# Context products in plain fp32, and ten modulation dots in one buffer ahead of the scan stage

## The chip, the cores and the metric

One Trainium2 chip, one core of it. Times are microseconds (us) of device time; the time of a kernel is the median of its runs. Engines by their names in the profile: PE is TensorE, PEld its weight loads, DVE is VectorE, ACT is ScalarE, SP is the engine on whose queue every transfer of this kernel is issued.

## The reference, cut to what matters

A diffusion backbone of two layers over 1024 latent tokens of width 1024, with 256 context tokens. Layer 0 mixes tokens with a bidirectional gated recurrence (RG-LRU), layer 1 with a short convolution; each is followed by a gated feed-forward. What matters here is the start of layer 0:

```python
sm, cm, gm, sf, cf, gf = adaln(c, ada_w[l], ada_b[l])        # silu(c) @ w + b, six vectors of 1024
smc, cmc, ... = adaln(c_ctx, ada_w[l], ada_b[l])
hl = modulate(rms_norm(x, norm_mix_g[l]), sm, cm)
hc = modulate(rms_norm(h_ctx, norm_mix_g[l]), smc, cmc)
ul = seq_conv(hl @ w_x, ...);  uc = seq_conv(hc @ w_x, ...)   # hc @ w_x: the context products
a, b = rglru_coeffs(u, w_r, b_r, w_i, b_i, lam)              # two small products per block of 256 channels
h_t = a_t * h_{t-1} + b_t                                    # context first, then latent, both directions
yl = (gelu(hl @ w_gate) * (h_fwd + h_bwd)) @ w_out
```

The modulation vectors are products of one vector with 12 x 1024 columns of 1024 weights: 96 groups of 128 results. Each group is one DVE instruction here, a dot product of a 128x1024 tile of weights with the broadcast vector.

## The kernel before

All products work on 128x128 blocks. A full-precision product is made of three passes in fp32r: each operand is split into a high part (ACT rounds it into an fp32r tile) and a low part (DVE subtracts the high part), and `mm` (L436) issues high x high, high x low, low x high into the same PSUM bank. Weights come as 512 KB transfers into raw buffers (three, `raw0`, until the feed-forward opens a fourth) and are split into six slots of 512 columns, `wh` and `wl`. There are four PSUM bank pairs, handed out in turn by `bank` (L208).

The program is a list of units. `run_units` (L369) walks it; ahead of each unit it issues the loads for which a raw buffer is free and the splits for which slots are free, in order of first use. A raw buffer counts as free once its split is recorded. `Plan` (L52) records every instruction and, at each `flush` (L121), writes out all that it recorded since the last one: it plays the instructions through with its own costs, takes at each step the one with the earliest due time among those that could start, and so sets the order in each engine's queue. Engines run their queues in order. So nothing of a later flush comes ahead of anything of an earlier flush on the same engine. The due time of an instruction that nobody in its flush needs is the summed PE cost at its place plus 60 (L134). PE's own order is that of the program.

The stages around the change, by the words of `ORDER` (L45):

- `start` (L567): the first products, with waits on the input.
- `g2`, `shift`, `g3`, `norm`, `g4`, `g5`: gate products of 1024 columns, 48 PE instructions each. `shifts` (L678) convolves three early products into `u` (`u_new`, L732); one of these products, with number 0, stands in `acct`, the 128x1024 tile that later holds square sums and, from here on, serves modulation dots. Then it runs the softplus of the recurrence (`sp` tile).
- `ctx`: `ctx_apply` (L709) makes the modulated context, as `hch` and `hcl`; then eight times `wx_ctx` (L744): 24 PE instructions of 256 columns and a convolution (`conv_a`, L718) of one ACT and three DVE instructions into `uc`.
- `mx`: `open_mx` (L772) flushes, closes the context tiles and opens `mx`, the working tile of the scans.
- `us0`, `e6`, `x4`, `r0`, `d3`, `x5`, `d2`, `r1`, ...: `u_split` (L727) splits `u` and `uc` into `uh`, `ul`; `x4` to `x7` are the remaining products with w_x; `r0` to `r7` (`ri`, L778) are the gates of the recurrence: 60 products that read `uh` and `ul`, then a chain of ACT and DVE instructions and three scans on DVE. `e` and `d` with a number are that many modulation dots (`ahead_dots`, L864): a load of 512 KB and one DVE instruction. `e` puts each in another part of `mx`, `d` puts it in `acct`, so that the load of the next waits for the dot before it.
- Then the output product, the feed-forward, layer 1 and its feed-forward, up to the end. The flush that closes the scan stage is that of `open_ffn` (L910).

Of the kernel before, what the change touches and what calls it, by code (L numbers as in the profile page):

```python
# [8 lines left out]
F32 = mybir.dt.float32  # L9
F32R = mybir.dt.float32r  # L10
AF = mybir.ActivationFunctionType
ALU = mybir.AluOpType

P = 128
D = 1024
KD = 8
SEQ = 1024
HALF = 512
CTX = 256
# [11 lines left out]
for _n, _w in _VEC:  # L31
# [10 lines left out]
DOTS = (0, 0, 0, 1, 1, 2, 2, 2)  # L42


ORDER = ("g2 shift g3 norm g4 g5 ctx mx us0 e6 x4 r0 d3 x5 d2 r1 d2 us2 x6 d1 r2 d1 x7 d1 r3 d1 us4 d1 r4 d1 g6 r5 "  # L45
         "us6 g7 r6 r7")

TABLE = {AF.Silu: (AF.Silu, AF.Tanh), AF.Gelu_apprx_tanh: (AF.Gelu_apprx_tanh, AF.Tanh), AF.Sqrt: (AF.Sqrt,),
         AF.Exp: (AF.Exp, AF.Tanh), AF.Tanh: (AF.Exp, AF.Tanh)}
# [134 lines left out]
def hybrid_kernel(ctx: ExitStack, tc: tile.TileContext, out, xs, cs, c, cc, ada, vecs,  # L184
                  ident, w0, wx, wg, wo, wri, wbi, wbo, wup, wdn):
    nc = Plan(tc)
    V, S, T, G = nc.vector, nc.scalar, nc.tensor, nc.gpsimd
# [28 lines left out]
    def stt(o, a, s, b, op0=ALU.mult, op1=ALU.add, eng=None):  # L216
        (eng or V).scalar_tensor_tensor(out=o, in0=a, scalar=s, in1=b, op0=op0, op1=op1)
# [10 lines left out]
    def act(o, i, f, bias=0.0, scale=1.0):  # L228
        S.activation(o, i, f, bias=bias, scale=scale)
# [24 lines left out]
    x = xp.tile([P, KD, SEQ], F32, tag="x", name="x")  # L254
# [25 lines left out]
    wslots = [(wh0, wl0, i) for i in range(6)]  # L280

    def unit(fn, *keys):
        units.append((fn, keys))
        return len(units) - 1

    class Raw:

        def __init__(self, src, after=-1, pool="raw"):
            self.src, self.after, self.pool, self.left, self.tile = src, after, pool, 0, None

    class Item:

        def __init__(self, key, raws, n, prep, after=-1):
            self.key, self.raws, self.n, self.prep, self.after = key, raws, n, prep, after
            for r in raws:
                r.left += 1

    items = {}

    def wsrc(key):  # L300
        kind = key[0]
        if kind in ("x", "xc"):
            return wx[key[1]]
        if kind == "g":
            return wg[key[1]]
        if kind == "o":
            return wo[key[1]]
        if kind == "ri":
            return wri[key[1]]
        if kind == "bo":  # L310
            return wbo[key[1]]
        return wdn[key[1], key[2], :, 2 * D:]
# [56 lines left out]
    def run_units(nside):  # L369


        stream, seen, last = [], {}, {}
        for i, (_, keys) in enumerate(units):
            for k in keys:
                if k not in seen:
                    seen[k] = i
                    stream.append(items[k] if k in items else weight_item(k))
                    for _ in range(nside(k)):
                        if side:
                            src, dst, bt, eng = side.pop(0)  # L380
                            stream.append(Item(None, [Raw(src)], 0, lambda sl, raws, dst=dst, bt=bt, eng=eng:
                                               dot(dst, raws[0].tile, bt, eng)))
                last[k] = i
        loads = {"raw": [], "s": []}
        for it in stream:
            for r in it.raws:
                if r not in loads[r.pool]:
                    loads[r.pool].append(r)
        free, pos = [True] * 64, 0
        occ, rp = {n: {} for n in loads}, dict.fromkeys(loads, 0)  # L390
        live, np_ = {}, 0
        for i, (fn, keys) in enumerate(units):
            while True:
                moved = False
                for name, todo in loads.items():
                    tiles = raw0 + more.get("raw", []) if name == "raw" else more.get("stage", [])
                    while todo and todo[0].after < i:
                        at = [(rp[name] + j) % len(tiles) for j in range(len(tiles))]
                        at = [j for j in at if j not in occ[name] or not occ[name][j].left]
                        if not at:  # L400
                            break
                        r = todo.pop(0)
                        r.tile = tiles[at[0]]
                        if len(r.src.shape) == 3:
                            nc.sync.dma_start(r.tile.rearrange("p (a b) -> p a b", a=r.src.shape[1]), r.src)
                        else:
                            nc.sync.dma_start(r.tile[:, :r.src.shape[-1]], r.src)
                        occ[name][at[0]] = r
                        rp[name], moved = at[0] + 1, True
                while np_ < len(stream):  # L410
                    it = stream[np_]
                    if it.after >= i or any(r.tile is None for r in it.raws):
                        break
                    n = len(wslots)
                    at = [(pos + j) % n for j in range(n)]
                    at = [j for j in at if j % max(it.n, 1) == 0 and all(free[j:j + it.n])]
                    if not at:
                        break
                    sl = list(range(at[0], at[0] + it.n))
                    if it.n:  # L420
                        pos = (at[0] + it.n) % n
                    for j in sl:
                        free[j] = False
                    for r in it.raws:
                        r.left -= 1
                    live[it.key] = (it.prep([wslots[j] for j in sl], it.raws), sl)
                    np_, moved = np_ + 1, True
                if not moved:
                    break
            fn(*[live[k][0] for k in keys if k[0] != "act"])  # L430
            for k in keys:
                if last[k] == i:
                    for j in live.pop(k)[1]:
                        free[j] = True

    def mm(ps, w, wi, rh, rl, start, stop, **o):  # L436

# [5 lines left out]
    def mmk(ps, w, rhi, rlo, s):  # L443
        n = len(rhi)
        for k in range(n):
            mm(ps[:, s], w, slice(k * P, (k + 1) * P), rhi[k][:, s], rlo[k][:, s], k == 0, k == n - 1)

    def call(fn, *a):
        unit(lambda: fn(*a))
# [97 lines left out]
    cpx = ExitStack()  # L547
    cp = cpx.enter_context(tc.tile_pool(name="cp", bufs=1))
    cs6 = cp.tile([P, 6, CTX], F32, tag="cs6", name="cs6")
    hch = cp.tile([P, KD, CTX], F32R, tag="hch", name="hch")  # L550
    hcl = cp.tile([P, KD, CTX], F32R, tag="hcl", name="hcl")
    xc = cp.tile([P, KD, CTX], F32, tag="xc", name="xc")
    ccb = cp.tile([P, D], F32, tag="ccb", name="ccb")
    uc = up.tile([P, KD, CTX], F32, tag="uc", name="uc")
# [154 lines left out]
    def ctx_apply():  # L709
        make_ab(1, modc, 0, 0, 1, "norm_mix_g")  # L710
        A, B = ab(1)
        for k in range(KD):
            u = cs6[:, 2 + k % 4]
            stt(u, xc[:, k], A[k], rc[0], ALU.mult, ALU.mult)
            act(hch[:, k], u, AF.Identity, bias=B[k])
            stt(hcl[:, k], u, B[k], hch[:, k].bitcast(F32), ALU.add, ALU.subtract)

    def conv_a(z, u, m):  # L718

        n = z.shape[-1]  # L720
        w = [vcol("a_conv_w", t * 8 + m) for t in range(4)]
        act(u, z, AF.Identity, bias=vcol("a_conv_b", m), scale=w[2])
        stt(u[:, 1:], z[:, :n - 1], w[1], u[:, 1:])
        stt(u[:, 2:], z[:, :n - 2], w[0], u[:, 2:])
        stt(u[:, :n - 1], z[:, 1:], w[3], u[:, :n - 1])
# [16 lines left out]
        unit(f, ("x", m))  # L742

    def wx_ctx(m):  # L744
        def f(w):
            z = bank()
            mmk(z, w, [hch[:, k] for k in range(KD)], [hcl[:, k] for k in range(KD)], slice(0, CTX))
            conv_a(z[:, :CTX], uc[:, m], m)
        unit(f, ("xc", m))

    def gate(m):
# [110 lines left out]
    mods = [mod_item(0, j) for j in range(16, 48)] + [mod_item(1, j) for j in range(48)]  # L862
# [9 lines left out]
    for o in ORDER.split():  # L872
        if o[0] == "g":
            gate(int(o[1]))
        elif o == "shift":
            call(shifts)
        elif o == "norm":
            call(ctx_rstd)
        elif o == "ctx":
            call(ctx_apply)  # L880
            for m in range(KD):
                wx_ctx(m)
        elif o == "mx":
            call(open_mx)
        elif o[:2] == "us":
            call(u_split, int(o[2]))
            call(u_split, int(o[2]) + 1)
        elif o[0] == "x":
            wx_lat(int(o[1]))
        elif o[0] == "e":  # L890
            call(ahead_dots, [mods.pop(0) for _ in range(int(o[1:]))],
                 lambda: mxp[0][:, NMX - 1 - ring("room", NMX), :D])
        elif o[0] == "d":
            call(ahead_dots, [mods.pop(0) for _ in range(int(o[1:]))])
        else:
            ri(int(o[1]))
# [548 lines left out]
```

## Time and profile before

| | us |
|---|---|
| median of 3 runs | 2080.49 (2080.05 to 2080.99) |
| the profiled execution's own time | 2082.59 |
| its span, first to last instruction | 2080.8 |
| PE busy in the span | 2036.8 (98%) |
| DVE busy | 1764.5 (85%) |
| ACT busy | 1049.3 (50%) |

A busy PE is one that has instructions in flight. The granted clock (PEclk) is the share of 2.4 GHz that PE was given; 0.5 is 1.2 GHz. "Idle before" is the time an engine stood still ahead of an instruction, with what ended it.

### The profile page before, as it was taken

The numbers are of one execution on the slowest core, as the hardware profiler recorded it, in microseconds if no ns is written. First come the engines' busy times: TensorE is split into PE (matmuls) and PEld (weight loads), VectorE is DVE, ScalarE is ACT, GpSimd is POOL, SyncE is SP. The second block draws the span as 40 slices with busy tenths as digits, with TensorE's granted clock in tenths as the row PEclk, the third lists the DMA queues.
The fourth block names the chain that finished last, engine by engine and source line by source line (L and its number), as shares of the span: only waits on it lengthen the run. The fifth ranks groups of instructions, "written<-read, shape, count | busy, mean of one in ns | idle before, by whom it ended". The sixth has DMA issues, their size and how long they took to land.

```text
span 2080.8 us, 25029 instructions
## 1 busy us (share of the span) xinstructions
PE 2036.8 (98%) x9218; PEld 1681.5 (81%) x9218; DVE 1764.5 (85%) x2624; ACT 1049.3 (50%) x1574; POOL 0.2 (0%) x4
## 2 busy tenths in 40 slices
PE   8899989999999999999999999999999999999998
PEld 6688877787888888878888788888888888878888
DVE  7998999979888888798769988858988887688867
ACT  6366878546544444535255433435644444464345
POOL 0000000000000000000000000000000000000000
PEclk9999999999999999999999999999999999999999
DMA  7544222551334455565361345652243443474345
GB/s 298 185 169 162 71 81 84 193 167 48 126 132 157 156 174 173 174 199 162 95 194 66 114 164 197 231 192 75 83 136 128 142 137 108 137 236 142 111 140 164
DMA packets 103418, 307.05 MB, mean 148 GB/s; under 512 B 10368, under 2 KB 14720, under 8 KB 103168
## 3 DMA queue, kind: packets, MB, share of 16 engines
q1 hardware_dynamic: 103296, 305.46, 44.6%
q8 instruction: 72, 1.18, 0.2%
q14 instruction: 50, 0.41, 0.1%
HBM read 248.80 MB, written 56.62 MB: 147 GB/s over the span
## 4 chain that ended last, share of the span: by engine, by line
PE 84%; DVE 9%; ACT 4%; DMA 2%; issue 1%; SPq 0%; DVEq 0%; ACTq 0%
PE banks L165 84%; ACT mx L165 2%; DVE x L165 2%; DVE mx L165 2%; DVE u L165 2%; DVE bl L165 2%; DMA x<-in_xs 1%; DVE wl L165 1%; DMA s<-bd 1%; ACT L165 1%; ACT bh L165 1%; DMA raw<-in_wg 0%; DVE uc L165 0%; DVE ul L165 0%; DVE acct L165 0%
## 5 line engine op out<-in xcount | busy, mean ns | idle before, releaser
L165 PE MATMUL banks<-bl,wh 128*128 128x512 f32 (+1 forms) x2720 | 1052.2, 387 | 11.0 <-DVE bl L165 10.9
L165 PE MATMUL banks<-bh,wh 128*128 128x512 f32 (+1 forms) x2720 | 1054.3, 388 | 3.2 <-ACT wh L165 1.6
L165 PE MATMUL banks<-bh,wl 128*128 128x512 f32 (+1 forms) x2720 | 1051.0, 386 | 2.6 <-DVE wl L165 2.5
L165 PEld LDWEIGHTS banks<-bl,wh 128*128 128x128 f32 x2720 | 511.6, 188 | 124.7 <-DVE bl L165 21.6
L165 PEld LDWEIGHTS banks<-bh,wh 128*128 128x128 f32 x2720 | 511.8, 188 | 109.0 <-ACT wh L165 2.0
L165 PEld LDWEIGHTS banks<-bh,wl 128*128 128x128 f32 x2720 | 511.6, 188 | 108.1 <-DVE wl L165 7.3
L165 ACT ACTIVATE wh<-raw 128x512 fp32r<-128x512 f32 (+2 forms) x386 | 275.6, 717 | 475.0 <-PE banks L165 394.7
L165 DVE TENSOR_TENSOR wl<-raw,wh 128x512 fp32r<-128x512 f32 (+2 forms) x386 | 303.2, 794 | 60.4 <-ACT wh L165 56.9
L165 DVE SCALAR_TENSOR_TENSOR x<-banks,mod,x 128x512 f32<-128x512 f32 (+1 forms) x184 | 132.6, 726 | 93.3 <-PE banks L165 92.3
L165 ACT ACTIVATE s<-banks 128x512 f32<-128x512 f32 x174 | 103.8, 596 | 195.0 <-PE banks L165 191.8
L165 ACT ACTIVATE wh<-s 128x512 fp32r<-128x512 f32 x216 | 135.5, 628 | 110.4 <-DVE s L165 63.7
L165 DVE TENSOR_TENSOR wl<-s,wh 128x512 fp32r<-128x512 f32 x216 | 148.5, 688 | 38.6 <-ACT wh L165 34.9
L165 DVE TENSOR_TENSOR s<-s,banks 128x512 f32<-128x512 f32 x158 | 107.8, 683 | 37.4 <-PE banks L165 36.9
L165 DVE SCALAR_TENSOR_TENSOR x<-s,vec,x 128x504 f32<-128x504 f32 x132 | 96.4, 740 | 10.2 <-ACT x L165 9.0
L165 DVE SCALAR_TENSOR_TENSOR acct<-acct,cb 128x1024 f32<-128x1024 f32 x69 | 84.1, 1218 | 4.5 <-DMA acct<-in_ada 4.5
L165 PE MATMUL banks<-uh,wh 128*128 128x512 f32 (+1 forms) x192 | 70.8, 369 | 8.1 <-ACT mx L165 7.0
L165 PE MATMUL banks<-ul,wh 128*128 128x512 f32 (+1 forms) x192 | 70.5, 367 | 3.1 <-DVE ul L165 3.1
L165 PE MATMUL banks<-uh,wl 128*128 128x512 f32 (+1 forms) x192 | 70.2, 366 | 0.0
L165 ACT ACTIVATE bh<-s 128x512 fp32r<-128x512 f32 x88 | 51.5, 624 | 35.3 <-DMA s<-bd 34.0
L165 ACT ACTIVATE bh<-x,cols 128x512 fp32r<-128x512 f32 x64 | 45.1, 721 | 42.1 <-DVE cols L165 27.3
L165 DVE TENSOR_TENSOR x<-x,s 128x512 f32<-128x512 f32 x90 | 61.0, 686 | 0.8
L165 DVE TENSOR_TENSOR bl<-s,bh 128x512 fp32r<-128x512 f32 x88 | 57.2, 684 | 5.0 <-ACT bh L165 5.0
(154 smaller groups left out, 1702.0 us busy)
## 6 DMA issues: line engine op xcount, KB each, us to landing
raw<-in_wup SPq DMA_DIRECT2D x92, 512.0 KB, 3.6
acct<-in_ada SPq DMA_DIRECT2D x69, 512.0 KB, 3.5
bd<-x SPq DMA_DIRECT2D x48, 512.0 KB, 3.2
s<-bd SPq DMA_DIRECT2D x44, 512.0 KB, 4.5
raw<-in_wdn SPq DMA_DIRECT2D x32, 512.0 KB, 4.4
raw<-in_wdn SPq DMA_DIRECT2D x40, 384.0 KB, 3.4
raw<-in_wbi SPq DMA_DIRECT2D x26, 512.0 KB, 4.1
u<-in_ada SPq DMA_DIRECT2D x24, 512.0 KB, 4.6
```

Of the source, the lines that this page charges most:

```text
L165: getattr(getattr(self.tc.nc, e), op)(*a, **k)
```

## The change

The context products are no longer split. `hc` is one fp32 tile in place of `hch` and `hcl`; the weights are read by PE from the raw buffer, eight fp32 instructions per product in place of 24 in fp32r, and the raw buffer is held until the product is done. In `ORDER`, ten dots move from behind `mx` to ahead of it: one behind `g4`, one behind `g5`, one behind each of the eight context products, all in `acct`. Behind `mx` the 19 dots become 9: `e6` becomes `e3`, `d3` goes, the dots behind `x5` become one, those behind `r1` go, the one behind `r3` goes.

```diff
-ORDER = ("g2 shift g3 norm g4 g5 ctx mx us0 e6 x4 r0 d3 x5 d2 r1 d2 us2 x6 d1 r2 d1 x7 d1 r3 d1 us4 d1 r4 d1 g6 r5 "
-         "us6 g7 r6 r7")
+ORDER = "g2 shift g3 norm g4 d1 g5 d1 ctx mx us0 e3 x4 r0 x5 d1 r1 us2 x6 d1 r2 d1 x7 d1 r3 us4 d1 r4 d1 g6 r5 us6 g7 r6 r7"
...
                     for r in it.raws:
-                        r.left -= 1
-                    live[it.key] = (it.prep([wslots[j] for j in sl], it.raws), sl)
+                        r.left -= not it.hold
+                    live[it.key] = (it.prep([wslots[j] for j in sl], it.raws), sl, it.raws if it.hold else [])
...
             for k in keys:
                 if last[k] == i:
-                    for j in live.pop(k)[1]:
+                    _, sl, held = live.pop(k)
+                    for j in sl:
                         free[j] = True
+                    for r in held:
+                        r.left -= 1
...
-    hch = cp.tile([P, KD, CTX], F32R, tag="hch", name="hch")
-    hcl = cp.tile([P, KD, CTX], F32R, tag="hcl", name="hcl")
+    hc = cp.tile([P, KD, CTX], F32, tag="hc", name="hc")
...
             stt(u, xc[:, k], A[k], rc[0], ALU.mult, ALU.mult)
-            act(hch[:, k], u, AF.Identity, bias=B[k])
-            stt(hcl[:, k], u, B[k], hch[:, k].bitcast(F32), ALU.add, ALU.subtract)
+            act(hc[:, k], u, AF.Identity, bias=B[k])
...
         def f(w):
             z = bank()
-            mmk(z, w, [hch[:, k] for k in range(KD)], [hcl[:, k] for k in range(KD)], slice(0, CTX))
+            for k in range(KD):
+                T.matmul(z[:, :CTX], w[:, k * P:(k + 1) * P], hc[:, k], start=k == 0, stop=k == KD - 1)
             conv_a(z[:, :CTX], uc[:, m], m)
+        items["xc", m] = Item(("xc", m), [Raw(wx[m])], 0, lambda sl, rs: rs[0].tile, hold=True)
         unit(f, ("xc", m))
...
             for m in range(KD):
                 wx_ctx(m)
+                call(ahead_dots, [mods.pop(0)])
```

## Rows read from the trace of the kernel before

**Rows 1.** Stretches: length, busy PE, PEld, DVE, ACT, POOL; granted clock, DMA share, GB/s.

```profile
146.80:169.80 23.00, 23.00 (x193) 23.00 (x192) 20.61 (x32) 12.58 (x16) 0.00 (x0) 1.00 0.49 160
...
205.00:231.00 26.00, 25.49 (x124) 21.43 (x123) 25.79 (x25) 19.37 (x21) 0.00 (x0) 1.00 0.19 61
231.00:287.60 56.60, 50.25 (x241) 41.69 (x239) 56.01 (x58) 46.78 (x47) 0.00 (x0) 0.96 0.24 77
287.60:320.00 32.40, 32.40 (x147) 27.36 (x148) 31.53 (x30) 25.27 (x28) 0.00 (x0) 0.90 0.25 81
320.00:358.30 38.30, 33.95 (x168) 28.46 (x166) 36.85 (x39) 36.11 (x37) 0.00 (x0) 1.00 0.26 86
...
395.00:2080.00 1685.00, 1671.66 (x7502) 1380.88 (x7500) 1400.50 (x2148) 788.33 (x1279) 0.00 (x0) 1.00 0.45 147
```

**Rows 2.** The chain that ended last: start, us, what; its pieces from 100 on.

```profile
109.91 84.78 PE banks L165 x464
...
287.60 31.98 PE banks L165 x144
```

**Rows 3.** PE in order of time: first context product, then x4, then r0.

```profile
146.79 0.28 PE L165 MATMUL banks<-hch,wh 128*128 128x256 f32 x1
...
169.83 0.40 PE L165 MATMUL banks<-bh,wh 128*128 128x512 f32 x1
...
180.74 0.39 PE L165 MATMUL banks<-uh,wh 128*128 128x512 f32 x1
```

**Rows 4.** PE in order of time around the one fp32 product of 256 columns.

```profile
124.59 0.59 PE L165 MATMUL banks<-cs,ones 128*128 128x256 f32 x2
...
125.25 0.40 PE L165 MATMUL banks<-bl,wh 128*128 128x512 f32 x1
125.48 0.39 PE L165 MATMUL banks<-bh,wl 128*128 128x512 f32 x1
```

**Rows 5.** DVE in order of time, up to the convolution's last read of `acct`.

```profile
128.02 1.27 DVE L165 SCALAR_TENSOR_TENSOR u<-acct,vec,u 128x1022 f32<-128x1022 f32 x1
...
132.48 1.67 DVE L165 SCALAR_TENSOR_TENSOR cs<-xc,cols,cs 128x256 f32<-128x256 f32 x4
...
138.23 2.35 DVE L165 TENSOR_TENSOR wl<-raw,wh 128x1024 fp32r<-128x1024 f32 x2
...
146.49 1.28 DVE L165 SCALAR_TENSOR_TENSOR u<-acct,vec,u 128x1023 f32<-128x1023 f32 x1
```

**Rows 6.** Groups of DVE instructions from 100 to 180: busy us, mean ns.

```profile
L165 DVE SCALAR_TENSOR_TENSOR hcl<-cs,cols,hch 128x256 fp32r<-128x256 f32 x8 | 3.6, 481 | 0.1
```

**Rows 7.** DMA issues from 140 to 180: count, size, median us to landing.

```profile
raw<-in_wx SPq DMA_DIRECT2D x8, 512.0 KB, 4.3
```

**Rows 8.** DMA issues from 190 to 360, the same columns.

```profile
acct<-in_ada SPq DMA_DIRECT2D x12, 512.0 KB, 3.4
```

**Rows 9.** DVE in order of time behind `open_mx`.

```profile
173.57 2.35 DVE L165 TENSOR_TENSOR ul<-u,uh 128x1024 fp32r<-128x1024 f32 x2
...
177.86 1.22 DVE L165 SCALAR_TENSOR_TENSOR mx<-mx,cb 128x1024 f32<-128x1024 f32 x1 [1.27 <-DMA mx<-in_ada]
...
195.92 1.22 DVE L165 SCALAR_TENSOR_TENSOR acct<-acct,cb 128x1024 f32<-128x1024 f32 x1
```

**Rows 10.** Instructions on `acct` in two stretches: length, busy PE, PEld, DVE, ACT.

```profile
231.00:287.60 56.60, 0.00 (x0) 0.00 (x0) 6.84 (x12) 0.00 (x0) 0.96 0.24 77
...
320.00:358.30 38.30, 0.00 (x0) 0.00 (x0) 4.90 (x8) 0.00 (x0) 1.00 0.26 86
```

**Rows 11.** PE in order of time behind a gap in the scan stage.

```profile
287.60 0.79 PE L165 MATMUL banks<-uh,wh 128*128 128x512 f32 x1 [2.65 <-ACT mx L165]
288.19 0.63 PE L165 MATMUL banks<-ul,wh 128*128 128x512 f32 x1
...
292.46 0.63 PE L165 MATMUL banks<-uh,wl 128*128 128x512 f32 x1
```

**Rows 12.** What PE waited for from 200 to 400: us in total, times, longest.

```profile
PE banks L165 <- ACT mx L165: 7.0, 2, 4.3
```

More of the change, by code (lines that the diff above doesn't have):

```diff
@@ L291, in hybrid_kernel, with __init__ @@
     class Item:
-        def __init__(self, key, raws, n, prep, after=-1):
-            self.key, self.raws, self.n, self.prep, self.after = key, raws, n, prep, after
+        def __init__(self, key, raws, n, prep, after=-1, hold=False):
+            self.key, self.raws, self.n, self.prep, self.after, self.hold = key, raws, n, prep, after, hold
             for r in raws:
@@ L301, in wsrc @@
         kind = key[0]
-        if kind in ("x", "xc"):
+        if kind == "x":
             return wx[key[1]]
```

## The prediction

> **What bounds the kernel now.** I read the busy time by stretch first, since a share over 2080 us mixes stages [rows 1]. From 395 on PE is busy 1671.7 of 1685.0 us at full clock, and the change touches nothing there; I carry that part over unshifted in length. Ahead of it there are two regimes. The chain of waits runs through PE alone from 109.91 to 194.7 [rows 2]: gates, context products, x4, and the products of r0. In the context stretch, 146.8 to 169.8, PE is busy throughout and DVE 20.6 of 23.0 us [rows 1]. From 205 DVE is the fullest engine: 25.79 of 26.0, 56.01 of 56.6, 31.53 of 32.4 and 36.85 of 38.3 us up to 358.3 [rows 1]. PE stands still there and then runs at a lower clock. It waits 7.0 us for ACT [rows 12], but the ACT instructions it waits for stand behind DVE work in turn. From 287.6 to 319.6 the chain is PE's again [rows 2]. So work taken off DVE counts from 231 to 287.6 and from 320 to 395, and less between.
>
> **The change part by part.**
>
> *The fp32 products.* The 192 instructions of the context products take 169.83 - 146.79 = 23.04 us, 0.12 each [rows 3]. The price of a plain fp32 product of 256 columns is in the trace once: it is issued as two instructions at 124.59; the fp32r product behind it has its successor at 125.25, and such a 512-column product takes 0.23 from start to start (125.25 to 125.48), so the fp32 product took 125.25 - 0.23 - 124.59 = 0.43 us [rows 4]. 64 of them are 27.5 us, 4.5 more than before. Bounds: 0.43, and 0.46 if each of the two instructions costs the 0.23 of a 512-column product: 29.4 us, +6.4. I take 4.5, the product's own row. It lies on the path, since PE is full and nothing covers it.
> The Trainium skill, FP8 and Floating Point Precision, section TensorE Precision Notes, says true FP32 takes four passes through the array; at the 0.12 us of a pass here that would be 64 x 4 x 0.12 = 30.7 us, +7.7. The row gives 3.6 passes of 0.12, and I keep the row.
>
> *What is no longer split.* Eight `hcl` instructions, 3.6 us of DVE [rows 6], and eight weight splits of 1.14 us, the mean step of the pair at 138.23 [rows 5], 9.1 us; ACT loses as many. This is work beside a full PE: worth nothing by itself. It makes room for ten dots of 1.15 us.
>
> *The held buffers.* A weight for a context product can be loaded only when the product three before it is done. Two products (6.9 us) lie between that and its use; a load lands in 4.3 us here [rows 7]. Hidden by 2.6 us; if a dot's load stands ahead of it on SP's queue, the cover is gone (a rival below).
>
> *The ten dots ahead of `mx`.* This part decides. All ten use `acct`, so each is a load, a wait for its landing, a dot of 1.2 us, and only then the next load. A load takes 3.4 us to land where the queues are quiet [rows 8] and 4.3 in this stretch [rows 7]. So one dot takes 4.65 to 5.6 us; I take 5.0, as the queues are quieter behind the last context product. Ten take 50 us (46.5 to 56).
> The chain can start when `acct` is last read by the early convolution, at 146.49 to 147.7 now [rows 5]. That instruction comes so late because its due time is late: the context tiles, the weight splits and the softplus go first. Of what stands between 132.48 and it, two weight splits (2.3) and the low parts `hcl` (8 x 0.4 = 3.2) go, so it ends at about 142.2. The due times that the new dots give it, worked back over ten links of the planner's own costs, still lie behind those of the softplus, so I see no reason for it to move further ahead. Bounds: 129.3, where it would stand directly behind the convolution step before it (at 128.02 [rows 5]), and 147.7.
> So the last dot ends at 142.2 + 50 = 192.2. The context products end at 146.8 + 27.5 = 174.3 and x4 at 174.3 + 10.9 = 185.2 (10.9 from 169.83 to 180.74 [rows 3]).
> Behind the waiting dots stands everything that `open_mx` separates: its flush puts all ten ahead of the whole scan stage in DVE's queue. First there is the split of `u` into `ul`, now at 173.57 [rows 9], 1.2 us for each half; r0 needs it for its second product. So PE can start r0 at 192.2 + 1.2 = 193.4 in place of 180.7: 12.7 us later, of which 4.5 are the fp32 products and 8.2 a new stall. Bounds by the two prices and the two starts: from no stall (129.3 + 46.5 = 175.8, well ahead of 185.2) to a start of r0 at 147.7 + 56 + 1.2 = 204.9. On SP the ten loads stand ahead of those for the three dots in `mx`, whose results nobody in the scan stage reads, and among those for x5 and the gates of r2, which are used only after r0: I cost that at nothing, as r0 itself is later.
> The Trainium skill, DMA: Bandwidth & Descriptors, section Anatomy of one DMA, gives 2.0 us plus bytes / 436e3 for one transfer, measured for those that GpSimd issues, by which 512 KB land in 3.2 us. The sum by it would be 4.4 a dot, the last at 186.2, and a stall of 2.2. The rows of this stretch, 4.3, are above that and decide.
>
> *The clock.* Behind a wait of 2.65 us, PE ran its 512-column products at 0.43 us from start to start in place of 0.23, from 288.19 to 292.5 and beyond, which is the 1.2 GHz level [rows 11]; that stretch has a mean of 0.90 [rows 1], and 0.10 x 32.4 x 2 = 6.5 us at half speed lose 3.2. The new stall is longer, so r0 starts slow: +2.7, between 0 and 3.2.
>
> *The dots that leave the scan stage.* 19 become 9. Before 205 now stand seven (the six of `e6` from 177.86, one in `acct` at 195.92 [rows 9]); of the other twelve, six stand from 231 to 287.6 and four from 320 to 358.3, each two instructions [rows 10]. After the change three stand in `mx` and one behind x5, which all fit where DVE waits for r0; five go with x6 to r4. So the stretch from 231 to 287.6 loses its six, 6.8 us, and that from 320 on one, 1.2: 8.0 us off a DVE that is 99% and 96% busy there. With a shorter wait ahead of 287.6, I count half of the clock lost behind it, 1.4 more. Bounds: 3 us, if ACT (46.8 of 56.6 us busy [rows 1]) takes the bound, to 11.2, with all of the lost clock back. I take 9.4.
>
> *Sum:* 12.7 + 2.7 - 9.4 = +6.0 us. On the profiled execution's own time, 2082.59, that is 2088.6; this execution stood 2.1 us above the median, so on the median 2080.49 + 6.0 = 2086.5.
>
> **The rivals.**
>
> *The dots are done in time (faster).* If the early convolution leaves `acct` before about 136 and a dot takes 4.75 us, the last ends by 184, the split of `u` is there when x4 ends at 185.2, and no stall arises. Then +4.5 - 9.4 = -4.9: 2075.6. It decides at that start: 184 - 47.5 = 136.5. For it: the second last step of that convolution runs at 128.02 [rows 5], and DVE loses 12.7 us of work ahead of 173. Against it: nothing gives the step an earlier due time, and DVE stood full up to there.
>
> *The relief is swallowed (slower still).* ACT's chain of tables and activations sets the scan stage, DVE's freed time becomes idle time. For it: PE's longest waits end with ACT [rows 12], ACT is at 36.1 of 38.3 us from 320 on [rows 1]. Then 12.7 + 2.7 - 3 = +12.4: 2092.9.
>
> *The weights come late.* SP issues in order, so a load of a held buffer behind a dot's load waits up to a dot's 5.0 us, 2.4 more than the cover; five loads make PE late by up to 12 us in the context products. The dots run on meanwhile, so r0 would start at 197.2, 3.8 later than forecast: +9.8, 2090.3.
>
> **How the numbers follow.** 0.2% is 4.2 us, about what can be told from no change. The forecast has a chance of 0.57, with its own range 2080 to 2093 (a last dot between 188 and 197, relief between 6 and 11): 0.38 of it slower, 0.17 within, 0.02 faster. The dots in time: 0.27 (0.21 faster, 0.06 within). Relief swallowed: 0.10, all slower. Weights late: 0.06 (0.04 slower, 0.02 within). Faster 0.23, within 0.25, slower 0.52. The range reaches from below the first rival, 2074, to above the second, 2095.
>
> **What would show it.** Right: ten dots on `acct` in DVE's queue at steps of about 5 us, the first between 141 and 148, the last well behind the context products' end; DVE idle for DMA of `acct` from 176 to 192; the first `uh` product of PE at about 193, behind a gap of some 8 us that DVE's `ul` ends, and half clock behind it; no context product's gap for DMA of `raw`; context products 27.5 us long; from then to 395 a stretch shorter by 6 to 11 us. Wrong: the last dot ahead of 185, or r0 without a gap; then the sign turns. A stretch that doesn't shorten makes it worse than forecast.

## The result and the profile after

| | before | after |
|---|---|---|
| median, us | 2080.74 | 2096.15 |
| the profiled execution's own time | 2082.59 | 2097.40 |
| its span | 2080.8 | 2095.5 |
| PE busy | 2036.8 | 2037.7 |
| DVE busy | 1764.5 | 1753.4 |
| ACT busy | 1049.3 | 1042.1 |

The ratio is 1.0072, with a 95% interval of 1.0058 to 1.0087: 15.0 us slower (12 to 18), where +6.0 was predicted. One of the four runs after (2554 us, at a granted clock of 0.75) is left out of the ratio; the others are 2094.2 to 2097.4. Below, a ratio is turned into microseconds by 2080.

First the stretches of after that answer to [rows 1], with the same columns: the context products, then the stretch that answers to 205 to 231, and the rest of the kernel.

```profile
144.30:171.80 27.50, 27.50 (x130) 24.18 (x128) 16.44 (x32) 6.02 (x9) 0.00 (x0) 1.00 0.62 214
...
224.50:250.30 25.80, 25.29 (x123) 21.27 (x122) 25.59 (x25) 19.37 (x21) 0.00 (x0) 1.00 0.19 62
...
409.50:2094.50 1685.00, 1672.00 (x7503) 1380.82 (x7501) 1400.59 (x2147) 788.63 (x1279) 0.00 (x0) 1.00 0.45 147
```

The context products are 27.5 us of full PE, 4.5 more than before, and the last 1685 us have not changed. So all of the loss lies between 144 and 409. DVE in time order, the view of [rows 5] and [rows 9]; the brackets are the idle time before an instruction and what ended it:

```profile
139.42 1.28 DVE L164 SCALAR_TENSOR_TENSOR u<-acct,vec,u 128x1023 f32<-128x1023 f32 x1
...
144.23 1.23 DVE L164 SCALAR_TENSOR_TENSOR acct<-acct,cb 128x1024 f32<-128x1024 f32 x1 [2.17 <-DMA acct<-in_ada]
...
155.49 1.52 DVE L164 SCALAR_TENSOR_TENSOR uc<-banks,vec,uc 128x255 f32<-128x255 f32 x3 [1.94 <-ACT uc L164]
156.93 1.22 DVE L164 SCALAR_TENSOR_TENSOR acct<-acct,cb 128x1024 f32<-128x1024 f32 x1
...
168.55 1.22 DVE L164 SCALAR_TENSOR_TENSOR acct<-acct,cb 128x1024 f32<-128x1024 f32 x1 [1.18 <-DMA acct<-in_ada]
...
185.62 1.23 DVE L164 SCALAR_TENSOR_TENSOR acct<-acct,cb 128x1024 f32<-128x1024 f32 x1 [4.41 <-DMA acct<-in_ada]
...
195.44 1.22 DVE L164 SCALAR_TENSOR_TENSOR acct<-acct,cb 128x1024 f32<-128x1024 f32 x1 [4.02 <-DMA acct<-in_ada]
...
196.59 2.35 DVE L164 TENSOR_TENSOR ul<-u,uh 128x1024 fp32r<-128x1024 f32 x2
...
290.76 1.22 DVE L164 TENSOR_TENSOR wl<-raw,wh 128x1024 fp32r<-128x1024 f32 x1
291.90 2.35 DVE L164 TENSOR_TENSOR ul<-x,uh 128x1024 fp32r<-128x1024 f32 x2
```

These are the last reading of `acct` by the early convolution; the first, third, fifth, eighth and tenth of the ten dots, and the convolution ahead of the third, which waits for ACT's reading of its product; then the split that r0 needs and, far behind, that of r2 with a weight split ahead of it. `acct` is free at 140.6, the last dot ends at 196.6: 5.6 us per dot. Directly behind it in DVE's queue comes r0's split. PE in time order, the view of [rows 3] and [rows 11]:

```profile
144.34 1.89 PE L164 MATMUL banks<-hc,raw 128*128 128x256 f32 x8
...
171.77 0.58 PE L164 MATMUL banks<-bh,wh 128*128 128x512 f32 x1
...
184.76 0.50 PE L164 MATMUL banks<-uh,wh 128*128 128x512 f32 x1 [1.65 <-ACT uh L164]
197.87 0.79 PE L164 MATMUL banks<-ul,wh 128*128 128x512 f32 x1 [12.60 <-DVE ul L164]
198.46 0.63 PE L164 MATMUL banks<-uh,wl 128*128 128x512 f32 x1
...
202.71 0.40 PE L164 MATMUL banks<-uh,wh 128*128 128x512 f32 x1
...
293.17 0.50 PE L164 MATMUL banks<-ul,wh 128*128 128x512 f32 x1 [3.45 <-DVE ul L164]
...
371.54 0.50 PE L164 MATMUL banks<-uh,wh 128*128 128x512 f32 x1 [3.47 <-ACT mx L164]
...
381.37 0.79 PE L164 MATMUL banks<-bh,wl 128*128 128x512 f32 x1 [3.49 <-DVE wl L164]
```

r0's first product waits 1.65 us, its second 12.60. The eleven products from 197.87 to 202.71 take 4.84 us, 0.43 from start to start once PE runs (the 1.2 GHz level), where 0.23 each would be 2.5.

Three rows of before answer to r0's second product and to the waits at 293.17 and 381.37; the wait of before at 287.60 [rows 11] has no counterpart after.

```profile
180.96 0.39 PE L165 MATMUL banks<-ul,wh 128*128 128x512 f32 x1
...
273.91 0.79 PE L165 MATMUL banks<-ul,wh 128*128 128x512 f32 x1 [3.11 <-DVE ul L165]
...
367.27 0.50 PE L165 MATMUL banks<-bh,wl 128*128 128x512 f32 x1 [1.13 <-DVE wl L165]
```

The balance of the two profiled executions, with times counted from the first context product (146.79 before, 144.34 after, so that the 2.45 us by which the second execution is early there stay out):

- r0's second product: 180.96 before, so 34.2 after the start; after the change 53.5. That is +19.4: 4.5 for the fp32 products and 14.9 of new stall (14.25 of it the two waits).
- Slow clock behind the stall: 4.84 - 2.5 = +2.3.
- The wait for `ul` in r2: 127.1 before, 148.8 after: +21.7. Up to here the scan stage has given back nothing.
- The wait for `wl` behind the gates: 220.5 and 237.0: +16.5, so 5.2 came back between the two, where the wait of 2.65 us at 287.60 and its half clock [rows 11] are gone. The other waits there nearly cancel: that for ACT is shorter (3.47 us in place of 4.35) and not followed by half clock, that for `wl` is longer (3.49 in place of 1.13). To the end 0.6 more is lost: +17.1.
- Less the 2.45 at the start: 14.7, the difference of the spans.

### The profile page after: what moved, and what is told of

Read it like the earlier page. It is cut to its first block, busy times and chain, and to the rows that moved or that the text cites. A ratio compares the mean times of both kernels' runs of the same rounds, so it can differ in the third digit from the quotient of the medians.

```text
span 2095.5 us, 24857 instructions
## 1 busy us (share of the span) xinstructions
PE 2037.7 (97%) x9154; PEld 1679.8 (80%) x9154; DVE 1753.4 (84%) x2608; ACT 1042.1 (50%) x1566; POOL 0.2 (0%) x4
## 4 chain that ended last, share of the span: by engine, by line
PE 84%; DVE 9%; ACT 3%; DMA 2%; issue 1%; SPq 0%; DVEq 0%; ACTq 0%
PE banks L164 84%; DVE u L164 2%; DVE x L164 2%; ACT mx L164 1%; DVE bl L164 1%; DVE mx L164 1%; DMA acct<-in_ada 1%; DVE wl L164 1%; DVE acct L164 1%; DMA s<-bd 1%; DVE ul L164 1%; ACT bh L164 0%; ACT L164 0%; DMA x<-in_xs 0%; DVE uc L164 0%
## 5 line engine op out<-in xcount | busy, mean ns | idle before, releaser
L164 ACT ACTIVATE wh<-raw 128x512 fp32r<-128x512 f32 (+2 forms) x378 | 267.1, 709 | 469.1 <-PE banks L164 373.3
L164 DVE TENSOR_TENSOR wl<-raw,wh 128x512 fp32r<-128x512 f32 (+2 forms) x378 | 293.8, 786 | 60.0 <-ACT wh L164 56.6
```

What stands on the lines that cost most here:

```text
L164: getattr(getattr(self.tc.nc, e), op)(*a, **k)
```

## The experiments

All times are ratios to runs of the kernel before on the same chip. `Plan` orders the queues anew for every kernel, so each run shows its edit together with the order that `Plan` found for it.

**The fp32 products alone** (e1): the changed kernel with the order of before and no dot among the context products.

```diff
-ORDER = "g2 shift g3 norm g4 d1 g5 d1 ctx mx us0 e3 x4 r0 x5 d1 r1 us2 ..."
+ORDER = "g2 shift g3 norm g4 g5 ctx mx us0 e6 x4 r0 d3 x5 d2 r1 d2 us2 ..."
...
-                call(ahead_dots, [mods.pop(0)])
```

> The changed kernel with the order of before: plain fp32 context products and held raw buffers, but all 19 dots behind mx as before. Theory A (the chain of ten dots in one buffer makes the loss): no stall ahead of r0; what is left is 64 fp32 products at 0.43 us in place of 23.0 us, less the splits that DVE and ACT no longer do: 2083 to 2086, 2 to 5 over before. Theory B (fp32 products and held buffers make the loss: weights late, PE waiting inside the context products or at x4): 2090 or more.

Measured: 1.0046 [1.0031, 1.0061], +9.6 us: far more than the 4.5 of the products. That is the size of theory B, but PE waits neither inside the context products nor at x4. ACT in time order shows where from, and PE what it cost:

```profile
176.00 1.06 ACT L165 ACTIVATE wh<-raw 128x1024 fp32r<-128x1024 f32 x1 [3.18 <-DMA raw<-in_wri]
181.72 1.06 ACT L165 ACTIVATE wh<-raw 128x1024 fp32r<-128x1024 f32 x1 [4.66 <-DMA raw<-in_wri]
182.69 1.99 ACT L165 ACTIVATE uh<-u 128x1024 fp32r<-128x1024 f32 x2
```

```profile
183.78 0.50 PE L165 MATMUL banks<-uh,wh 128*128 128x512 f32 x1 [0.67 <-ACT uh L165]
185.23 0.50 PE L165 MATMUL banks<-ul,wh 128*128 128x512 f32 x1 [0.95 <-DVE ul L165]
...
186.37 0.79 PE L165 MATMUL banks<-ul,wh 128*128 128x512 f32 x1 [0.17 <-DVE ul L165]
```

While two of the three raw buffers are held by context products, the weights of x4 and of r0's two gates pass one after another through the third. The second gate's load is issued at 178.35, when the first gate's split has ended on DVE, and its split on ACT ends at 182.7. It belongs to the flush ahead of the scan stage, so it stands ahead of `uh` in ACT's queue. `uh` and `ul` come late, PE stands three times for 1.8 us together, and its clock falls behind that.

**The dots alone** (e2): the kernel before, split products kept, with the new order and the ten dots.

```diff
                 wx_ctx(m)
+                call(ahead_dots, [mods.pop(0)])
```

> The kernel before, with its split context products, and the ten dots moved as in the change. Theory A: DVE is fuller ahead of the scan stage than with fp32 products and frees the buffer later (147.7 in place of 140.6 us), so the last dot ends at 200 to 207, r0 starts 20 to 27 later than before, and with the slow clock behind it and some 5 us given back in the scan stage the time is 2098 to 2106, worse than the whole change. Theory B: 2077 to 2084, since the products are the old ones and the scan stage has ten dots less.

Measured: 1.0134 [1.0118, 1.0149], +27.9 us, somewhat more than theory A gave, and not for its reason: `acct` comes free early enough for its load to be issued at 142.71. But DVE is full with splits and convolutions here, so that the first dot stands at 163.6 and not at 144.2. First and last dot on DVE, then r0 on PE:

```profile
163.62 1.22 DVE L164 SCALAR_TENSOR_TENSOR acct<-acct,cb 128x1024 f32<-128x1024 f32 x1
...
208.70 1.22 DVE L164 SCALAR_TENSOR_TENSOR acct<-acct,cb 128x1024 f32<-128x1024 f32 x1 [3.92 <-DMA acct<-in_ada]
```

```profile
211.12 0.80 PE L164 MATMUL banks<-ul,wh 128*128 128x512 f32 x1 [29.88 <-DVE ul L164]
```

**The ten dots left out** (e3): the changed kernel, ten of the 96 modulation columns are not computed and stay zero.

```diff
-... g4 d1 g5 d1 ctx mx ...
+... g4 g5 ctx mx ...
...
+    del mods[:10]
...
-                call(ahead_dots, [mods.pop(0)])
```

> The changed kernel with the ten moved dots left out altogether (their ten columns of modulation stay zero, so this part of the result is not computed). Theory A: the stall of 12.6 + 1.7 us ahead of r0 and the 2.4 us of slow clock behind it go, the scan stage keeps what it gained: 2096.2 - 16.7 = 2079.5, between 2077 and 2082. Theory B: at most 5 us better than the changed kernel, 2091 or more.

Measured: 1.0013 [1.0003, 1.0022], +2.7 us, just above the range of theory A. The chain of dots is worth 15.0 - 2.7 = 12.3 us. Against e1, which has all 19 dots behind `mx`, ten dots fewer give 6.9.

**Ten dots in three buffers** (e4): the changed kernel, each early dot in one of two new tiles or `acct`, in turn.

```diff
+    dt = cp.tile([P, 2, D], F32, tag="dt", name="dt")
...
+    def early():
+        i = ring("early", 3)
+        return dt[:, i] if i < 2 else acct.rearrange("p a b -> p (a b)")
...
-                call(ahead_dots, [mods.pop(0)])
+                call(ahead_dots, [mods.pop(0)], early)
```

> The changed kernel, but the ten dots take turns in three buffers (two new tiles in the space that the low parts of the context left, and the buffer of the square sums), so a load need not wait for the dot just before it. Everything else is as in the change. Theory A: the last of the ten ends ahead of 180, r0 starts behind x4 at about 183, and the time is that of the ten left out within 3 us: 2078 to 2083. Theory C (the dots cost what they cost because DVE and the queues are full there, wherever they land): 2088 or more.

Measured: 1.0018 [1.0008, 1.0028], +3.7 us, as with the dots left out: the ten instructions and their 5 MB cost 1.0 us beside e3, which the intervals do not tell from nothing. That each load waits for the dot before it is what costs: 15.0 - 3.7 = 11.3 us.

**The relief alone** (e5): the kernel before without the ten dots that leave the scan stage; again ten columns stay zero.

```diff
-... mx us0 e6 x4 r0 d3 x5 d2 r1 d2 us2 x6 d1 ...
+... mx us0 e3 x4 r0 x5 d1 r1 us2 x6 d1 ...
...
+    del mods[:10]
```

> The kernel before, split products and all, with the same ten dots left out and nine kept behind mx (their columns of modulation stay zero, so this part of the result is not computed). It prices the relief of the scan stage without fp32 products. From the runs so far the relief is 2090.4 - 2083.5 = 6.8. Theory A: 2080.4 - 6.8 = 2073.6, between 2071 and 2076. Rival (the relief only takes back what fp32 products and late weights had cost): 2078 or more.

Measured: 0.9977 [0.9968, 0.9987], -4.8 us, about half of the 9.4 predicted. PE in time order; its first context product is at 143.68 here:

```profile
270.77 0.80 PE L164 MATMUL banks<-ul,wh 128*128 128x512 f32 x1 [3.44 <-DVE ul L164]
...
359.49 0.79 PE L164 MATMUL banks<-bh,wl 128*128 128x512 f32 x1 [3.49 <-DVE wl L164]
```

Counted from that product the first wait stands at 127.1, to a tenth where it stood before, the second at 215.8 instead of 220.5. It is the pattern of the balance above, without any of the rest of the change.

**Own tiles for the context weights** (e7a): e1 with the context weights in three tiles that are free there, so that no raw buffer is held.

```diff
+    ctw = cp.tile([P, 2, D], F32, tag="ctw", name="ctw")
...
-        items["xc", m] = Item(("xc", m), [Raw(wx[m])], 0, ...
+        items["xc", m] = Item(("xc", m), [Raw(wx[m], cstart[0], "c")], 0, ...   # "c": ctw[:, 0], ctw[:, 1], x[:, 6]
```

> The fp32 products with all 19 dots behind mx, as in the run of fp32 alone (2090.4), but the context weights get three tiles of their own (two in the space that the low parts left, one in a free slot of x), so no raw buffer is held and the weights of x4 and of the gates of r0 need not follow one another through a single one. Theory D (the held buffers delay the gate weights, and their splits stand ahead of the first of the scan stage in the queues of ACT and DVE): r0 starts right behind x4 at 183 and without a slow clock, 2083 to 2086. Rival (the fp32 products themselves and the order that the planner then finds cost the 10 us): 2088 or more.

Measured: 1.0015 [1.0006, 1.0025], +3.1 us. r0 starts at 185.33 with no wait, 38.5 us behind the first context product: the 33.95 of before and 4.57. So the fp32 products, less what their missing splits give back, cost 3.1, and the held buffers alone 9.6 - 3.1 = 6.5 (the two intervals leave 3 to 10). PE in time order:

```profile
185.33 0.39 PE L165 MATMUL banks<-uh,wh 128*128 128x512 f32 x1
...
370.53 0.50 PE L165 MATMUL banks<-bh,wl 128*128 128x512 f32 x1 [1.24 <-DVE wl L165]
```

e7a has three buffers more than e1, so 6.5 is the price of holding the shared ones against adding others. Counted from the first context product, r0's twelfth product stands at 45.1 in e1 and 41.0 here: 4.1 of the 6.5 come from the waits of r0 and the slow clock behind them. The rest lies in later waits of the scan stage and was not taken apart.

**Own tiles, and the early dots in two buffers** (e7): the changed kernel with the tiles of e7a and, of the early dots, every other one in a free slot of `x`.

```diff
...
+    def early():
+        i = ring("early", 2)
+        return x[:, 7] if i < 1 else acct.rearrange("p a b -> p (a b)")
```

> The changed kernel with both causes taken away: own tiles for the context weights, and the ten dots in turn in two buffers (the one of the square sums and a free slot of x). Theory A with D: no stall ahead of r0, the gain of the scan stage kept: 2083.7 - 4 = about 2079.5, between 2077 and 2082, at or just below before. Without D: 2082 to 2086 as with three buffers.

Measured: 1.0005 [0.9995, 1.0015], +1.0 us, not to be told from before. Beside e7a that is 2.1 less: the relief, with whatever the ten early dots still cost taken off, and within the intervals none.

**Own tiles, the chain kept** (e10): the changed kernel with the edit of e7a alone.

```diff
-        items["xc", m] = Item(("xc", m), [Raw(wx[m])], 0, ...
+        items["xc", m] = Item(("xc", m), [Raw(wx[m], cstart[0], "c")], 0, ...
```

> The changed kernel, with the weights of the context products in three tiles of their own, so that the raw buffers are not held; the ten dots stay one behind another in acct. Theory (both mechanisms act, but the later one ends the wait): the chain of dots decides when r0 starts, and the 7.6 us of the held buffers lie under it. What the held buffers can still give is a shorter chain, since SP's held weight loads no longer stand ahead of acct's: between 5.0 and 5.6 us per dot, last dot at 191 to 197, r0's second product at 192 to 198: 2090 to 2096.5. Rival (the two costs add): 2096.2 - 7.6 = 2088.6 or less, with r0 at about 190.

Measured: 1.0065 [1.0051, 1.0078], +13.5 us; what the rival gave, 2088.6, is 1.0039 and outside. First, fifth and tenth dot on DVE, then r0 on PE:

```profile
143.90 1.22 DVE L164 SCALAR_TENSOR_TENSOR acct<-acct,cb 128x1024 f32<-128x1024 f32 x1
...
166.48 1.22 DVE L164 SCALAR_TENSOR_TENSOR acct<-acct,cb 128x1024 f32<-128x1024 f32 x1
...
190.42 1.23 DVE L164 SCALAR_TENSOR_TENSOR acct<-acct,cb 128x1024 f32<-128x1024 f32 x1 [4.01 <-DMA acct<-in_ada]
```

```profile
192.85 0.80 PE L164 MATMUL banks<-ul,wh 128*128 128x512 f32 x1 [10.41 <-DVE ul L164]
```

The two costs do not add: the chain ends last, and the held buffers lie under it. They lengthen it, though: from the first to the fifth dot a link is 6.1 us in the changed kernel and 5.6 here, from the fifth to the tenth 5.4 and 4.8.

**Five ahead, five back** (e6): the changed kernel with the dots behind g4, g5 and the first three context products, the other five behind `mx`.

```diff
-... mx us0 e3 x4 r0 x5 d1 r1 us2 x6 d1 r2 d1 x7 d1 r3 us4 ...
+... mx us0 e3 x4 r0 d1 x5 d2 r1 d2 us2 x6 d1 r2 d1 x7 d1 r3 d1 us4 ...
-                call(ahead_dots, [mods.pop(0)])
+                if m < 3:
+                    call(ahead_dots, [mods.pop(0)])
```

> The changed kernel with the dots behind g4, g5 and the first three context products only; the other five go back behind mx (behind r0, x5, r1 and r3). Theory (one chain of 5.6 us per link, harmless until it passes the end of x4): five links end at 144.2 + 28 = 172, ahead of the split of u, so r0 waits as in the kernel without dots (185 to 188) and only half of the relief of 6.8 us is lost: 2083.5 + 3.4 = 2086.9, 2085 to 2089. Rival (each early dot costs its share, as it stands in DVE's queue between convolutions and on SP's queue between loads): halfway between 2090.4 and 2096.2, 2093.

Measured: 1.0035 [1.0022, 1.0048], +7.3 us; the rival's 2093 is 1.0061 and outside. The fifth dot ends at 173, and r0's waits (0.96, 0.95 and 0.18 us) are nearly those of e1. So early dots don't cost their share each: a chain that ends ahead of x4 shows no cost. At how many dots it begins to cost was not tried.

**Ten early dots in three buffers beside the split products** (e8): e2 with `x[:, 6]`, `x[:, 7]` and `acct` in turn.

```diff
-                call(ahead_dots, [mods.pop(0)])
+                call(ahead_dots, [mods.pop(0)], early)
```

> The kernel before with its split products, and the ten dots moved as in the change, but in turn in three buffers (the one of the square sums and two free slots of x). If only the chain in one buffer is at fault: DVE is near full ahead of the scan stage (20.6 of 23.0 us in the context products), so ten dots delay its first split by some 8 us and r0 by 1 to 4; with the relief of 6.8 the time is 2075 to 2080. If DVE's room decides: 2084 or more, as r0 starts 8 or more late.

Measured: 0.9998 [0.9989, 1.0008]: 28 us better than e2 by the buffers alone, but no gain over before. Ten dots among DVE's splits push the last convolutions back. x4's first product on PE waits for one of them, and half clock follows:

```profile
169.22 0.47 PE L164 MATMUL banks<-bh,wh 128*128 128x512 f32 x1 [2.63 <-DVE uc L164]
```

r0 itself does not wait, but starts at 181.81, 38.4 us behind the first context product (143.39) and not 33.95, and that takes up the relief.

**Seven early dots beside the split products** (e9): as e8, with `e6` kept in `mx` and a dot behind the first seven context products only.

```diff
-ORDER = ("... ctx mx us0 e6 x4 r0 d3 x5 d2 r1 d2 us2 x6 d1 r2 d1 x7 d1 r3 d1 us4 ...")
+ORDER = "... ctx mx us0 e6 x4 r0 x5 d1 r1 us2 x6 d1 r2 d1 x7 d1 r3 us4 ..."
...
+                if m < 7:
+                    call(ahead_dots, [mods.pop(0)], early)
```

> The kernel before with its split products; the six dots behind us0 kept in mx, the six from d3 to the one behind r1 and the one behind r3 moved ahead of mx, each behind one of the first seven context products, in two unused quarters of x and in acct in turn. Theory (a dot that neither waits for the one before it nor stands ahead of the convolution that PE's next products need costs nothing, and the relief is that of ten dots left out, less what stays): relief of up to 5 us, less 1 to 2 us for convolutions delayed: 2075 to 2078, ratio 0.9975 to 0.9990. Rival (DVE is full, 20.6 of 23.0 us, beside the split products, so that seven dots of 1.2 us push uc and with it r0 late): 2079 to 2082.

Measured: 0.9982 [0.9973, 0.9991], -3.7 us: the one complete kernel here that beats the kernel before. DVE, three dots in a row that wait for nothing, and r0 on PE without a gap, 34.3 us behind the first context product (143.41):

```profile
160.60 1.22 DVE L164 SCALAR_TENSOR_TENSOR x<-x,cb 128x1024 f32<-128x1024 f32 x1
...
161.74 1.22 DVE L164 SCALAR_TENSOR_TENSOR acct<-acct,cb 128x1024 f32<-128x1024 f32 x1
...
162.89 1.22 DVE L164 SCALAR_TENSOR_TENSOR x<-x,cb 128x1024 f32<-128x1024 f32 x1
...
176.20 2.35 DVE L164 TENSOR_TENSOR ul<-u,uh 128x1024 fp32r<-128x1024 f32 x2
```

```profile
177.69 0.39 PE L164 MATMUL banks<-uh,wh 128*128 128x512 f32 x1
```

## Why the prediction was wrong

The direction and the main mechanism were right: a chain of ten loads and dots in one buffer, put by a flush ahead of r0's operands in DVE's queue. The sizes were not: +15.0 instead of +6.0, and just above the range. Three steps failed: the length of the chain (5.0 us for a dot, measured 5.6), the relief of the scan stage (9.4, measured 4.6 in the trace), and the held buffers, which were put at nothing and alone cost 6.5. By steps:

- *The fp32 products*: right in the profile (27.5 us, as taken from [rows 4]). By the runs they cost 3.1: in e7a r0 stands 4.6 later behind the first context product than before, and the wait for `wl` behind the gates only 3.2 (370.53 - 146.81 against 220.5). The Trainium skill, FP8 and Floating Point Precision, section TensorE Precision Notes, speaks of four passes, from which the estimate of 30.7 us was worked out; the trace has 27.5. This does not refute the four: 27.5 us over 64 x 4 passes are 0.107 each. It was the 0.12 of an fp32r pass that could not be carried over.
- *The ten dots ahead of `mx`*: the stall was put at 8.2 us and measured 14.9. Counted from the first context product the last dot was to end at 45.4 and ended at 52.3: 0.9 because `acct` came free later than thought, 6.0 because a dot took 5.6 us and not 5.0. Part of that is the held buffers: with them out of the way (e10) a dot takes 5.1 from the moment `acct` is free, r0's second product stands 4.2 us earlier, and the time falls by 1.5 (the intervals allow none). The end of the range, 5.6, stood in the prediction; the choice of 5.0 looked at the quiet end of the stretch, while the first dots stand in DVE's queue between convolutions that wait for their product (as at 155.49 above), and ahead of two of the last three DVE idles over 4 us for a landing beside the weight loads. The Trainium skill, DMA: Bandwidth & Descriptors, section Anatomy of one DMA, gives an estimate of 3.2 us per landing, from transfers that GpSimd issues; on SP's queue the median for `acct` was 4.2 here.
- *The held buffers*, costed at nothing: false. The step looked at the loads of the context weights alone, and those were in time: no context product waits. It did not follow what is queued behind them, x4's weight and r0's gates, through the one buffer left, nor the flush that puts their splits ahead of `uh`. Alone that costs 6.5 us (e1 against e7a). In the changed kernel the chain covers most of it.
- *The clock*: 2.7 predicted, 2.3 measured.
- *The dots that leave the scan stage*: put at 9.4; the trace shows 4.6, the runs 4.8 (e5), 6.9 (e3 against e1) and 2.1 (e7 against e7a, with the cost of the early dots in it). This term failed too. It counted DVE's removed work as time wherever DVE was full. But up to the wait for `ul` in r2 nothing is gained, though one dot and not four stands there: DVE does other work first, a weight split among it (290.76 above), and `ul` comes as late as before. What is gained is, in sum, one wait of PE, at 287.60, and the slow clock behind it. Two readings were off besides: from 287.6 to 320 PE is the fullest engine, not DVE (32.40 of 32.4 us [rows 1]), and of the six dots from 231 to 287.6 one starts at 230.49 and is there after too (250.12), so that stretch lost five.

Together, in the profile: +6.7 by the stall, +4.8 by the relief, -0.4 by the clock are the 11.1 us between 6.0 and 17.1. The steps by runs, each added to the one before: fp32 products +3.1 (e7a), held buffers +6.5 (e1), relief -6.9 (e3), chain of dots +12.3 (the changed kernel): 15.0.

Of the rivals, none came as described. The relief did shrink, but up to r2 it is DVE's `ul` that ends the wait and not ACT; for the stretch behind, where PE's wait at 371.54 ends with ACT, the rival's reason is not excluded. The weights and the dots did collide, but on the dots' side. How much of the 0.5 us that held buffers add to a link is SP's order, DVE's order or the sharing of transfers was not separated; the median landing of `acct`'s loads, 4.2 us in the changed kernel and 3.4 in e10, says that the transfers have a part in it.

## What to carry to other kernels

Work that is moved into a gap brings its buffer along: price a chain of load, use, next load at its full length against the first thing queued behind its end, and give it two or three buffers before counting its instructions. When a change holds a buffer longer, follow the loads behind the holder, not only the holder's own. Work taken off a full in-order engine is worth the waits that it ends, to be found one by one, and not its duration.

## What was not expected of the hardware

Ahead of the change all these kernels run the same PE instructions from the wait at 109 to the first context product. The stretch of before, of after and of e9, columns as in [rows 1]:

```profile
109.90:146.80 36.90, 36.89 (x153) 30.55 (x154) 34.84 (x70) 24.16 (x34) 0.00 (x0) 0.91 0.46 155
```

```profile
108.90:144.30 35.40, 35.40 (x152) 29.25 (x153) 31.61 (x64) 22.39 (x33) 0.00 (x0) 0.95 0.44 148
```

```profile
109.50:143.40 33.90, 33.89 (x152) 28.16 (x153) 32.97 (x63) 22.15 (x30) 0.00 (x0) 1.00 0.54 168
```

Behind the same wait of 2.4 us the granted clock was 0.91, 0.95 or 1.00, and the stretch 36.9, 35.4 or 33.9 us long. What makes the difference was not tried. A single profile is uncertain by up to 3 us for this alone, as much as several of the effects above; so positions were counted from the first context product, and the sizes taken from the runs.
